# One written order for the first two parts of an input projection

## The chip, the cores and the metric

The kernel runs on one core of one Trainium2 chip. The metric is the device time of one execution in microseconds (us). Three runs of the kernel before took 2344.2, 2344.32 and 2345.24 us.

The engines are called as the profile calls them: PE (TensorE), DVE (VectorE), ACT (ScalarE), POOL (GpSimd) and SP (SyncE, which here only issues DMAs).

## The reference, cut to what matters

One step of a two-layer network for two groups of 128 tokens each: context tokens and latent tokens. Both groups have D_MODEL = 2048 features and share all parameters. They differ in a conditioning vector, from which a shift, a scale and a gate per feature are made for every sub-layer. The first layer begins like this:

```python
mod = jax.nn.silu(cond) @ w_ada[l] + b_ada[l]
sh1, sc1, gt1, sh2, sc2, gt2 = jnp.split(mod[:, None, :], 6, axis=-1)
h = rmsnorm(x, g_norm_mix[l]) * (1 + sc1) + sh1
...
proj = h @ w_in
q_lat, ckv, k_rope = proj[..., :i0], proj[..., i0:i1], proj[..., i1:i2]
```

`rmsnorm` divides each token by the root of the mean of its squares. `w_in` has 2048 rows and 2880 columns. Attention, an output projection, a gated feed-forward network with a convolution and a second layer follow; the change touches them only in a helper and through the scheduler.

## The kernel before, in words

**Layout.** Features lie on the 128 partitions, tokens along the free axis: `x` is 16 chunks of 128 features by 256 tokens, the first 128 of which are the context group. Each f32 product is made of three: an operand is split into a high part (rounded to fp32r by a cast on ACT) and a low part (the difference, on DVE), and PE multiplies high by high, low by high and high by low. `split` (L242 to L245) does this for weights; its ACT cast is the group "wh" (L244) in the profile, its DVE difference the group "wl" (L245). `gemm` (L330) issues the three matmuls for each chunk of rows into one of three PSUM banks called `acc`.

**The in-projection** is in `mixer_ab` (L825). Its 2048 rows are taken in five parts: chunks 0 and 1 (part one), chunks 2 and 3 (part two), and then three parts of four chunks. Each part runs over 23 columns of 128 outputs (`part`, L936). Part one copies its sums to SBUF on ACT (L942), the others add theirs on DVE (L944). A column of parts one and two is six matmuls, a column of the later parts twelve. `Weights` (L249) loads tiles of 1 MB (2048 values on each partition) into one of three buffers called `raw`; a tile holds eight columns of part one or two, or four of a later part.

**Shift and scale** are vectors made on PE. A *unit* is 512 features of one of them: four tiles of 1 MB of `w_ada`, summed against the conditioning (`sum_rows`), then turned onto the partitions with transposes and finished on DVE. `ROWS` (L70) lists the units in order of need; `pump` and `row_step` (L560, L529) place them between the columns of a part at a rate (`RATE["in0"]` in part two). The first unit of the scale (j = 1) and of the shift (j = 0) is done in two halves of two tiles each, with 256 features (`load_half` L359, `half_unit` L366), so that part one can begin with its two chunks. Their tiles lie in two buffers called `araw`, which the later units use as well, or in `raw`.

**The start** (L1300 on). All constants are loaded with one DMA, then `x` in four pieces, then the tiles of the first halves. `stat_add` squares the 16 chunks one at a time on ACT and adds them on DVE; `stat_rstd` sums over the partitions on PE with a one-column matmul and takes the root (DVE and POOL, `rstd` L202). `diagonal` (L228) puts the factor on two diagonal matrices on DVE, and `spread` (L235) multiplies them with ones on PE, so that the factor stands on every partition. `modulate` (L591) makes the rows of a part from that: a product on DVE, scale and shift for one group on DVE and for the other on ACT, a cast on ACT and the low part on DVE or POOL.

**What sets the order.** The program is written in an order, and a scheduler places each engine's instructions by its own estimate of time, except those given to `keep_order`, which stay in the written order among themselves on their engine. `pe.in_turn` does this for all of PE's instructions while it is set; before, it is set for the third and fourth part only. Each engine then executes its own list strictly in turn, and SP issues DMAs in turn: a DMA that waits for a buffer holds up all behind it. In part one of before, the second halves' tiles are loaded behind column 2 and column 8 and summed behind columns 8 and 15 (`second_half`, L953), where the scheduler may shift them.

Of the kernel before, what the change touches and what calls it, by code (L numbers as in the profile page):

```python
# [37 lines left out]
    ("ident", 128), ("ones", 128), ("pick", 32), ("inv", 5), ("mhalf", 16),  # L38
    ("rch", 128), ("rsh", 128), ("rcm", 128), ("rsm", 128),
    ("cond", 32), ("bada", NL * 6 * KD),  # L40
    ("gmix", NL * KD), ("gffn", NL * KD), ("gfin", 16),
# [9 lines left out]
RATE = {"in0": 0.35, "in": 0.5, "in3": 0.25, "heads": 0.85, "out0": 0.75, "c": 0.43, "outc": 0.43}  # L51
# [37 lines left out]
def step_kernel(ctx: ExitStack, tc: tile.TileContext, A: dict):  # L89
# [54 lines left out]
    sp.dma_start(out=cst, in_=A["cst"])  # L144
# [17 lines left out]
    pool.memset(condw, 0.0)  # L162
    act.activation(condw[:, :, 0:2], C("cond").rearrange("p (k r) -> p k r", r=2), AF.Silu)
# [64 lines left out]
    def diagonal(r, cols):  # L228
        dg = T_(tmp, [P, 2 * T], "diag", bufs=1)
        for i, c in enumerate(cols):  # L230
            dve.tensor_scalar(out=dg[:, i * T:(i + 1) * T], in0=ident, scalar1=r[:, c:c + 1],
                              scalar2=None, op0=ALU.mult)
        return dg
# [15 lines left out]
    class Weights:  # L249
# [9 lines left out]
        def load(self):  # L259
            raw = T_(wpool, [P, 4, 512], "raw").rearrange("p g n -> p (g n)")  # L260
            sp.dma_start(out=raw, in_=self.src[self.at])
            self.at += 1
            return raw

        def ahead(self, pin):

            if not self.half:
                self.half = [self.load(), 0]
            raw, lo = self.half
            self.blocks += self.halves(raw, lo, pin)  # L270
            self.half = None if lo else [raw, 8]

        def halves(self, raw, lo, pin=lambda i: i):
            wh = T_(wpool, [P, 1024], "wh", F32R, bufs=4)
            wl = T_(wpool, [P, 1024], "wl", F32R, bufs=4)
            for at in range(0, 8, FINE):
                s = slice(at * P, (at + FINE) * P)
                split(wh[:, s], wl[:, s], raw[:, (lo + at) * P:(lo + at + FINE) * P], pin)
            return [(wh[:, b * P:(b + 1) * P], wl[:, b * P:(b + 1) * P]) for b in range(8)]

        def chunk(self):
            while len(self.blocks) < self.nblk:
# [3 lines left out]
                n = self.per  # L286
                if self.cycle:
                    n = min(n, self.cycle - self.at * n % (-(-self.cycle // n) * n))
                n *= self.nblk if self.per < TB else 1
                raw = T_(wpool, [P, 4, 512], "raw").rearrange("p g n -> p (g n)")  # L290
                sp.dma_start(out=raw[:, :n * P], in_=self.src[self.at, :, :n * P])
                self.at += 1
# [16 lines left out]
    def first_three(W, xh, xl, order, mid=None, fixed=False):  # L309
# [3 lines left out]
        raws = [W.load() for _ in range(3)]  # L313
# [45 lines left out]
    def load_half(j, h, tag):  # L359

        raws = [T_(wpool, [P, 4, 512], tag, **({"bufs": 2} if tag == "araw" else {})) for _ in range(2)]
        for t, raw in enumerate(raws):
            sp.dma_start(out=raw, in_=A["w_ada"][0, j, 0, 2 * h + t])
        return [raw.rearrange("p g n -> p (g n)").rearrange("p (b n) -> p b n", b=8) for raw in raws]

    def half_unit(j, h, raws, pin=lambda i: i):  # L366
        ps = T_(ppool["ada"], [P, 512], "ada", bufs=1)
        for k in range(KD):
            g = k % 4
            pin(pe.matmul(ps[32 * g:32 * g + 32, :NT], condw[:, k, :], raws[k // 8][:, k % 8],  # L370
                          start=(k < 4), stop=(k >= KD - 4), skip_group_check=True))
        am = T_(tmp, [P, 512], "am", bufs=1)
        act.copy(am[:, :NT], ps[:, :NT])
        pt = T_(ppool["ada"], [P, 512], "ada", bufs=1)
        for b in range(2):
            pe.transpose(pt[:, b * P:(b + 1) * P], am[:, b * P:(b + 1) * P], ident)
        at = slice(2 * h, 2 * h + 2)
        out = mod[:, 0, j, at]
        dve.tensor_reduce(out=out, in_=pt[:, :NT].rearrange("p (b g r) -> p b r g", b=2, g=4)[:, :, 0:2],
                          axis=AX.X, op=ALU.add)  # L380
        dve.tensor_tensor(out=out, in0=out, in1=vector("bada", 0, j, 0)[:, at], op=ALU.add)
        if j == 1:
            dve.scalar_tensor_tensor(out=scl[:, 0, 0, at], in0=out, scalar=1.0,
                                     in1=vector("gmix", 0, 0, 0)[:, at], op0=ALU.add, op1=ALU.mult)
        if h == 1:
            done.add((0, j, 0))
# [105 lines left out]
    def side_step():  # L492
# [11 lines left out]
        sp.dma_start(out=block, in_=A["w_ada"][u[0], u[1], u[2], k // 4][:, k % 4])  # L504
# [82 lines left out]
    def norm_scale(st):  # L587
        return spread(diagonal(stat_rstd(st, D), (0, 1)))

    def modulate(hx, rb, l, which, chunks, fixed=False):  # L590
# [26 lines left out]
        for c, h in lows:  # L617
            low(c, h)

# [45 lines left out]
    def modulated(st, l, which, W, u, to, rp):  # L665
# [18 lines left out]
        def stats():  # L684
            got["r"] = stat_rstd(st, D, att_bank)
            got["dg"] = diagonal(got["r"], (0, 1))

        def factor():
            got["rb"] = spread(got["dg"], bank=att_bank)
# [135 lines left out]
    def mixer_ab(hx, rb0, beside):  # L825
# [658 lines left out]
```

## Time and profile before

| What | Value |
|---|---|
| runs, median of 3 | 2344.32 us |
| span of the profiled execution (first to last instruction) | 2343.4 us |
| PE busy | 2301.2 us, 98% |
| weight loads of PE (PEld) busy | 2182.7 us, 93% |
| DVE busy | 1852.7 us, 79% |
| ACT busy | 1194.5 us, 51% |
| DMA | 612.98 MB, mean 262 GB/s |
| granted PE clock, mean | 0.996 |

The page shows the span of the profiled execution and no other time of its own; the runs are 0.8 to 1.8 us longer than the span. The page divides the span into 40 slices of 58.6 us, and gives the busy share of each engine in tenths. A table of windows gives the same for any stretch in microseconds, with the number of records in brackets. The chain of waits follows back from the last instruction what released each step. A busy PE is not PE at its peak: a matmul is shown longer than the distance to the next one, and a stream of them is read from the distance. "PE acc", "PE ada", "PE misc" are matmuls into the PSUM banks of that name: projections, sums of `w_ada` (and their transposes), and statistics.

### The profile page before, as it was taken

To read this page: it belongs to the slowest core of one execution; us is meant where nothing else is said; L and a number is where in the kernel's file an instruction comes from. 1 tells how busy PE (TensorE), PEld (TensorE's weight loads), DVE (VectorE), ACT (ScalarE), POOL (GpSimd) and SP (SyncE) were. 2 spreads that over 40 slices of the span, in tenths; PEclk is the share of its full clock that TensorE was granted. 3 is DMA by queue.
4 is the path that set the end of the run, shared out by engine and by line. 5 is a ranking of instruction groups with operands and counts; after the bars stand their busy time and mean duration, and the time that the engine had idled before them with its cause. 6 is when DMAs were issued, how large, how long until landed. Compare 5 with 4: busy or idle time off the path is not lost.

```text
span 2343.4 us, 47891 instructions
## 1 busy us (share of the span) xinstructions
PE 2301.2 (98%) x19650; PEld 2182.7 (93%) x19650; DVE 1852.7 (79%) x2879; ACT 1194.5 (51%) x1979; POOL 177.4 (8%) x250
## 2 busy tenths in 40 slices
PE   6999999999999999999999999999999999999997
PEld 4788768999999999999989999999999999999997
DVE  3569767789999999999988888797899755666654
ACT  4245545575553355555564444456655434555543
POOL 0002101210000000001130000023000000000011
PEclk9999999999999999999999999999999999999999
DMA  9988888677767777777778888777677555555553
GB/s 367 358 326 290 305 320 331 231 285 259 262 253 290 293 266 266 270 260 261 284 272 287 308 307 293 259 261 257 243 260 267 196 198 191 189 196 198 194 189 122
DMA packets 106524, 612.98 MB, mean 262 GB/s; under 512 B 11520, under 2 KB 19392, under 8 KB 38592
## 3 DMA queue, kind: packets, MB, share of 16 engines
q1 hardware_dynamic: 106304, 609.92, 71.8%
q8 instruction: 154, 2.52, 0.4%
q14 instruction: 66, 0.54, 0.1%
HBM read 605.12 MB, written 4.75 MB: 260 GB/s over the span
## 4 chain that ended last, share of the span: by engine, by line
PE 94%; DVE 2%; DMA 2%; ACT 1%; issue 1%; POOL 0%; SPq 0%; DVEq 0%; ACTq 0%; POOLq 0%
PE acc L104 86%; PE ada L104 4%; PE att L104 2%; DMA raw<-w_in_ab 1%; PE att L107 1%; DMA araw<-w_ada 1%; DVE wl L245 1%; PE misc L104 1%; PE ada L107 0%; ACT wh L244 0%; POOL block L736 0%; DVE aacc L488 0%; DVE x L1348 0%; DVE nt L603 0%; ACT p L787 0%
## 5 line engine op out<-in xcount | busy, mean ns | idle before, releaser
L244 ACT CAST wh<-raw 128x1024 fp32r<-128x1024 f32 (+2 forms) x824 | 795.2, 976 | 938.6 <-PE acc L104 742.9
L104 PE MATMUL acc<-hx,wh 128*128 128x256 f32 (+1 forms) x7296 | 1260.5, 278 | 5.7 <-ACT hx L613 4.3
L245 DVE TENSOR_TENSOR wl<-raw,wh 128x1024 fp32r<-128x1024 f32 (+2 forms) x824 | 919.1, 1132 | 302.1 <-ACT wh L244 296.9
L104 PEld LDWEIGHTS acc<-hx,wh 128*128 128x128 f32 x7296 | 1102.3, 188 | 39.0 <-issue 19.2
L104 PE MATMUL acc<-hx,wl 128*128 128x256 f32 (+1 forms) x3648 | 1011.4, 278 | 4.5 <-DVE wl L245 4.5
L104 PEld LDWEIGHTS acc<-hx,wl 128*128 128x128 f32 x3648 | 686.4, 188 | 9.8 <-DVE wl L245 5.5
L104 PE MATMUL acc<-g,wh 128*128 128x256 f32 x2816 | 478.9, 276 | 0.0
L104 PEld LDWEIGHTS acc<-g,wh 128*128 128x128 f32 x2816 | 424.0, 188 | 0.0
L104 PE MATMUL acc<-g,wl 128*128 128x256 f32 x1408 | 388.6, 276 | 0.0
L459 DVE CUSTOM_DVE_ANT_0 junk<-araw,condb 128x2048 f32<-128x2048 f32 x120 | 275.9, 2299 | 0.0
L104 PE MATMUL acc<-hxc,wh 128*128 128x256 f32 (+1 forms) x1536 | 267.5, 278 | 1.1 <-DVE hxc L740 1.1
L104 PEld LDWEIGHTS acc<-g,wl 128*128 128x128 f32 x1408 | 264.3, 188 | 0.0
L104 PEld LDWEIGHTS acc<-hxc,wh 128*128 128x128 f32 x1536 | 233.0, 188 | 1.8 <-DVE hxc L740 1.3
L104 PE MATMUL acc<-hxc,wl 128*128 128x256 f32 (+1 forms) x768 | 218.4, 284 | 0.0
L200 POOL TENSOR_TENSOR sqacc<-sqacc,sq 128x256 f32<-128x256 f32 x62 | 68.5, 1105 | 1512.9 <-ACT sq L196 1512.6
L488 DVE SCALAR_TENSOR_TENSOR aacc<-block,condw,aacc 128x512 f32<-128x512 f32 x240 | 170.9, 747 | 7.4 <-DMA block<-w_ada 7.2
L104 PEld LDWEIGHTS acc<-hxc,wl 128*128 128x128 f32 x768 | 144.7, 188 | 15.8 <-issue 11.3
L104 PE MATMUL ada<-araw,condw 128*32 128x512 f32 (+1 forms) x736 | 94.2, 591 | 13.8 <-DMA araw<-w_ada 13.8
L1242 ACT ACTIVATE cv<-acc,convw 128x256 f32<-128x256 f32 x170 | 94.8, 557 | 0.0
L755 DVE SCALAR_TENSOR_TENSOR x<-acc,mod,x 128x128 f32<-128x128 f32 x192 | 57.8, 343 | 41.7 <-PE acc L104 41.6
L1248 DVE SCALAR_TENSOR_TENSOR cv<-acc,convw,cv 128x254 f32<-128x254 f32 x170 | 81.4, 479 | 3.3
L1245 DVE SCALAR_TENSOR_TENSOR cv<-acc,convw,cv 128x254 f32<-128x254 f32 x170 | 80.7, 475 | 0.0
(224 smaller groups left out, 1404.6 us busy)
## 6 DMA issues: line engine op xcount, KB each, us to landing
raw<-w_up SPq DMA_DIRECT2D x176, 1024.0 KB, 4.8
araw<-w_ada SPq DMA_DIRECT2D x146, 1024.0 KB, 5.4
raw<-w_down SPq DMA_DIRECT2D x88, 1024.0 KB, 4.8
raw<-w_in_c SPq DMA_DIRECT2D x48, 1024.0 KB, 6.5
block<-w_ada SPq DMA_DIRECT2D x128, 256.0 KB, 5.3
raw<-w_in_ab SPq DMA_DIRECT2D x19, 1024.0 KB, 7.5
raw<-w_out_ab SPq DMA_DIRECT2D x16, 1024.0 KB, 7.4
raw<-w_out_c SPq DMA_DIRECT2D x16, 1024.0 KB, 6.2
```

The source lines that it names most:

```text
L104: return self.placed(nc.tensor.matmul(*a, **kw))
L107: return self.placed(nc.tensor.transpose(*a, **kw))
L200: eng.tensor_tensor(out=st["acc"], in0=st["acc"], in1=sq, op=ALU.add)
L244: pin(act.copy(out_hi, src))
L245: pin(dve.tensor_tensor(out=out_lo, in0=src, in1=out_hi.bitcast(F32), op=ALU.subtract))
L459: keep_order(dve.tensor_tensor_reduce(out=T_(feat["pool"], [P, D], "junk"), in1=feat["row"][:, c], in0=feat["raw"].rearrange("p g n -> p ( ...
L488: i = dve.scalar_tensor_tensor(out=acc[c], in0=block, scalar=condw[:, k, c:c + 1], in1=acc[c], op0=ALU.mult, op1=ALU.add)
L755: dve.scalar_tensor_tensor(out=x[:, c, s], in0=ps[:, s], scalar=mod[:, l, 3 * which + 2, c, g:g + 1], in1=x[:, c, s], op0=ALU.mult, op1=AL ...
L1242: pin(act.activation(y, ps, AF.Identity, scale=cw[:, 1, m:m + 1], bias=cw[:, 3, m:m + 1]))
L1245: pin(dve.scalar_tensor_tensor(out=y3[:, :, 1:], in0=p3[:, :, :T - 1], scalar=cw[:, 0, m:m + 1], in1=y3[:, :, 1:], op0=ALU.mult, op1=ALU.add))
L1248: pin(dve.scalar_tensor_tensor(out=y3[:, :, :T - 1], in0=p3[:, :, 1:], scalar=cw[:, 2, m:m + 1], in1=y3[:, :, :T - 1], op0=ALU.mult, op1=A ...
```

## The change

It rewrites the start and the first two parts of the in-projection.

- The fields of the constants are put in another order; 373 columns are loaded first, the other 1024 inside part one, behind column 10 (`late_constants`).
- A dummy Silu on ACT stands ahead of the real one.
- The squares are taken four chunks at a time: four ACT instructions of 128x1024 and three DVE additions of that size, and eight one-column matmuls where there were four.
- `diagonal` is gone. `spread` multiplies the factor, broadcast along its row as the stationary operand, with the identity: two matmuls of 128x128 in place of one of 128x256. All callers use it: the first norm, the latents' and keys' norms, the two places of `modulated`, and the last norm.
- `half_unit` becomes the class `HalfUnit` with separate steps (`sums` of a tile, `copy`, `turn`), all kept in order, its sums and its transposes in PSUM banks of their own.
- The rows of parts one and two are made in two steps: `scaled_rows` (product with the factor and with the scale, DVE) as soon as the scale is there, and `begin_row` (shift and cast in one ACT instruction per group, low part on DVE) once the shift is there.
- `Weights` gets `begin` (load ahead, in order) and `take`. The loads of `w_ada` and `w_in_ab` at the start are all kept in order on SP, and so are the blocks of `side_step`, which before could be loaded at any time.
- `pe.in_turn` is set from part one on. The second halves' tiles are summed behind columns 4 and 10 (scale) and 15 and 19 (shift); the loads of the shift's tiles stand behind the first two of these.
- `RATE["in0"]` is 0.42 in place of 0.35, and `pump` runs from column 20 of part one in place of 16.

The core of the diff:

```diff
-RATE = {"in0": 0.35, ...
+NEARLY = _AT["bada"][0] + 2 * KD
+RATE = {"in0": 0.42, ...
-    sp.dma_start(out=cst, in_=A["cst"])
+    sp.dma_start(out=cst[:, :NEARLY], in_=A["cst"][:, :NEARLY])
+
+    def late_constants():
+        keep_order(sp.dma_start(out=cst[:, NEARLY:], in_=A["cst"][:, NEARLY:]))
...
-    def spread(dg, cols=(0, 1), bank=bank):
+    def spread(r, bank=bank):
         ps = bank()
-        n = len(cols) * T
-        pe.matmul(ps[:, :n], ones, dg[:, :n], start=True, stop=True)
-        return ps[:, :n]
+        for g in range(2):
+            pe.matmul(ps[:, g * T:(g + 1) * T], r[:, g:g + 1].to_broadcast([P, P]), ident, start=True, stop=True)
+        return ps[:, :NT]
...
-                for h in range(2):
-                    W = Weights(A["w_in_ab"][3 * h:3 * h + 3], 2, 8, cycle=23)
-                    if h == 0:
-                        W.ahead(keep_order)
-                    modulate(hx, rb0, 0, 0, range(2 * h, 2 * h + 2))
-                    if h == 0:
-                        part(W, 0, 2, True, 0, second_half)
-                    else:
-                        part(W, 2, 2, False, RATE["in0"], until=4)
+                def second_half(c):
+                    if c == 0:
+                        W0.ahead(keep_order)
+                    elif c == 4:
+                        second["u"] = HalfUnit(1, 1, ppool["first"], att_bank)
+                        second["u"].sums(0, second[1][0])
+                        second[0] = load_half(0, 1, "araw", (0,))
+                    elif c == 10:
+                        second["u"].sums(1, second[1][1])
+                        second["u"].copy()
+                        second[0] += load_half(0, 1, "araw", (1,))
+                        halves.begin(2)
+                        late_constants()
+                    elif c == 11:
+                        second["u"].turn()
+                    elif c == 15:
+                        second["u"] = HalfUnit(0, 1, ppool["first"], att_bank)
+                        second["u"].sums(0, second[0][0])
+                        second["nt"] = scaled_rows(rb0, 2, 2)
+                    elif c == 19:
+                        second["u"].sums(1, second[0][1])
+                        second["u"].copy()
+                    elif c == 20:
+                        second["u"].turn()
+                        for i, h in enumerate(second["nt"]):
+                            begin_row(hx, h, 2 + i)
+                    if c >= 20:
+                        pump(RATE["in0"], until=4)
+
+                second[1] = load_half(1, 1, "araw", (0,))
+                W0.begin()
+                second[1] += load_half(1, 1, "araw", (1,))
+                W0.begin()
+
+                def first_half(c):
+                    if c == 20:
+                        rest.begin()
+
+                pe.in_turn = True
+                part(W0, 0, 2, True, 0, second_half)
+                part(halves, 2, 2, False, RATE["in0"], first_half, then=lambda: rows(1), until=4)
...
-        half_unit(1, 0, first[1], keep_order)
-        st = stat_init()
-        for c in range(KD):
-            stat_add(st, x[:, c], KD, dve)
-        rb0 = norm_scale(st)
-        half_unit(0, 0, first[0], keep_order)
+        W0 = Weights(A["w_in_ab"][0:3], 2, 8, cycle=23)
+        W0.begin(2)
+            for i in range(4):
+                to = sums if i == 0 else T_(sqs, [P, 4, NT], "sqs", bufs=2)
+                keep_order(act.activation(to, x[:, 4 * i:4 * i + 4], AF.Square))
+                if i:
+                    keep_order(dve.tensor_tensor(out=sums, in0=sums, in1=to, op=ALU.add))
+            unit = HalfUnit(1, 0, ppool["first"], att_bank)
+            unit.sums(0, first[1][0])
+            ps = bank()
+            for g in range(2):
+                for i in range(4):
+                    keep_order(pe.matmul(ps[:, g:g + 1], sums[:, i, g * T:(g + 1) * T], inv(D),
+                                         start=(i == 0), stop=(i == 3)))
+            r = rstd([ps[:, 0:2]], 2)
+        unit.sums(1, first[1][1])
+        unit.copy()
+        rb0 = spread(r)
+        unit.turn()
+        nts = scaled_rows(rb0, 0, 2)
+        unit = HalfUnit(0, 0, att_bank, att_bank)
+        for t in range(2):
+            unit.sums(t, first[0][t])
+        W0.ahead(keep_order, rows)
```

In the program as built, SP's list at the start reads: early constants, `x` (four), the scale's first two tiles (`araw`), the shift's first two (`raw`), part one's first tile in two pieces, the scale's third tile, part one's second, the scale's fourth, part one's third, the shift's third, the shift's fourth, part two's first tile in two pieces, the late constants, and four tiles of the next unit (two in `raw`, two in `araw`), then part two's second tile. PE's list has the sums of that unit's first tile, which is the third of the four on SP's list, ahead of part two's first column. From there on SP's list differs from the old one only in the place of the side blocks and in some neighbours changing places.

More of the change, by code (lines that the diff above doesn't have):

```diff
@@ L285, in chunk @@
                     continue
[L286 to L292, printed above, removed]
+                raw, n = self.take()
                 n0 = FINE if fine[0] else 8
@@ L312, in first_three @@
         pin = keep_order if fixed else lambda i: i
-        raws = [W.load() for _ in range(3)]
+        raws = [W.load()[0] for _ in range(3)]
         ps = [T_(pacc, [P, 512], "acc") for _ in range(3)]
@@ L357, in step_kernel, with load_half @@
     later = []
[L359 to L363, printed above, removed]
+    def load_half(j, h, tag, tiles=(0, 1)):
+        raws = [T_(wpool, [P, 4, 512], tag, **({"bufs": 2} if tag == "araw" else {})) for _ in tiles]
+        for t, raw in zip(tiles, raws):
+            keep_order(sp.dma_start(out=raw, in_=A["w_ada"][0, j, 0, 2 * h + t]))
@@ L364, in load_half @@
         return [raw.rearrange("p g n -> p (g n)").rearrange("p (b n) -> p b n", b=8) for raw in raws]
[L366 to L386, printed above, removed]
@@ L822, in head_ab, with mixer_ab @@
         split(hx[:, c, :NT], hx[:, c, NT:2 * NT], o[:, :NT])
-    def mixer_ab(hx, rb0, beside):
+    def mixer_ab(hx, rb0, W0, beside):
         l = 0
@@ L978, in rows @@
                     modulate(hx, rb0, 0, 0, range(4 * q, 4 * q + 4))
-                rows(1)
+                halves, more, second = Weights(A["w_in_ab"][3:6], 2, 8, cycle=23), {}, {}
+                rest = Weights(A["w_in_ab"][6:], 4, 4, cycle=23)
+                def second_half(c):
[36 more added lines that the diff above has]
+                part(halves, 2, 2, False, RATE["in0"], first_half, then=lambda: rows(1), until=4)
+                W = rest
                 for q in range(1, 4):
```

132 lines of the change are left out of this document (92 added, 40 removed).

## The prediction

> **What bounds the kernel now.** I read the page's 40 slices first, then a table of windows cut at the parts of the in-projection, then the chain of waits and the timeline inside the early windows.
>
> ```profile
> PE   6999999999999999999999999999999999999997
> DMA  9988888677767777777778888777677555555553
> ```
> ```profile
> 0.00:28.00 28.00, 11.26 (x78) 5.61 (x78) 10.71 (x31) 11.45 (x27) 1.41 (x6) 1.00 0.95 377
> 28.00:53.00 25.00, 23.63 (x206) 19.24 (x206) 9.81 (x18) 14.54 (x34) 1.22 (x1) 0.93 0.98 388
> 53.00:82.50 29.50, 26.52 (x212) 19.02 (x212) 19.00 (x47) 10.88 (x20) 2.72 (x3) 1.00 0.95 382
> 82.50:130.00 47.50, 45.54 (x357) 37.18 (x358) 28.15 (x52) 16.03 (x23) 1.63 (x2) 0.96 0.84 309
> 174.50:214.00 39.50, 38.86 (x328) 36.53 (x327) 39.38 (x83) 24.33 (x54) 10.70 (x11) 1.00 0.79 269
> 214.00:350.00 136.00, 134.60 (x935) 101.27 (x938) 101.49 (x254) 69.91 (x166) 18.11 (x47) 1.00 0.85 315
> 480.00:600.00 120.00, 120.00 (x1058) 120.00 (x1057) 108.80 (x148) 72.31 (x100) 0.00 (x0) 1.00 0.72 261
> ```
>
> The columns are the length, then busy us and records of PE, weight loads, VectorE, ScalarE and GpSimd, then granted clock, DMA share and GB/s. PE has no idle time from 480 to 600 us, and nine tenths or more in every slice but the first and last: only the start, the stages up to 480 us and the tail have time to give. The changed stretch is 0 to 82.5 us. There the DMA engines are 95 to 98% busy, so loads bound it together with PE's order. In 174.5 to 214 VectorE is full (39.38 of 39.50).
>
> **The change part by part.** First the prices of PE work, from the chain of waits and the timeline (an f32 matmul leaves two records there, so x16 is eight):
>
> ```profile
> 12.67 1.94 PE ada L104 x16
> 14.60 1.80 PE misc L104 x8
> 44.34 1.00 PE ada L104 x16
> 53.91 1.75 PE acc L104 x12
> 62.98 2.07 PE acc L104 x18
> 82.86 4.39 PE acc L104 x22
> ```
> ```profile
> 18.19 1.22 PE L104 MATMUL misc<-diag,cst 128*128 128x256 f32 x2
> 19.21 0.64 PE L107 MATMUL ada<-cst,am 128*128 128x128 f32 x2
> 21.01 3.64 PE L104 MATMUL ada<-raw,condw 128*32 128x256 f32 x32 [1.16 <-DVE mod L379]
> 28.34 1.01 PE L104 MATMUL acc<-hx,wh 128*128 128x256 f32 x3 [2.71 <-ACT hx L613]
> 31.15 0.58 PE L104 MATMUL acc<-hx,wh 128*128 128x256 f32 x1
> 59.23 1.04 PE L104 MATMUL ada<-raw,condw 128*32 128x512 f32 x8
> ```
>
> One tile of half-unit sums is 1.94 us when PE is slow and 1.00 when fast; a projection matmul is 0.115 fast (2.07/18) and 0.20 slow (4.39/22), so a column of parts one and two (six matmuls) is 0.69 or 1.2. One tile of a whole unit's sums is 1.0.
>
> Then the loads, from windows of 2.5 us and the view of the tile `araw`:
>
> ```profile
> 5.00:7.50 2.50, 0.00 (x0) 0.00 (x0) 0.43 (x1) 2.30 (x6) 0.00 (x0) 1.00 1.00 379
> 32.50:35.00 2.50, 2.50 (x29) 1.79 (x29) 0.00 (x0) 1.39 (x4) 0.00 (x0) 1.00 1.02 421
> 80.00:82.50 2.50, 0.72 (x7) 0.52 (x5) 2.50 (x7) 1.08 (x2) 0.62 (x1) 1.00 1.01 416
> 82.50:85.00 2.50, 2.14 (x10) 2.15 (x11) 1.77 (x3) 0.00 (x0) 0.00 (x0) 0.59 0.20 82
> ```
> ```profile
> DMA to landing us min/median/max: 4.8/9.4/13.2
> ```
>
> A full queue moves about 0.425 MB/us, so a tile of 1.05 MB takes 2.47 us of it. Alone, such a tile lands 4.8 us after its issue: 2.3 us more, of which I put 0.9 behind the data.
>
> *Start.* Only 373 of the 1397 columns of constants stand ahead of x. That is 0.52 MB or 1.2 us less, so the first half-unit tile lands at 11.4 where it landed at 12.67, and x, one tile ahead of it, at 9.0. The squares become four of 128x1024 on ScalarE and three such additions on VectorE; the trace has neither, and the nearest rows are casts and differences:
>
> ```profile
> 34.54 2.00 ACT L244 CAST wh<-raw 128x1024 fp32r<-128x1024 f32 x2 [0.63 <-DMA raw<-w_in_ab]
> 35.62 2.36 DVE L245 TENSOR_TENSOR wl<-raw,wh 128x1024 fp32r<-128x1024 f32 x2 [5.27 <-ACT wh L244]
> ```
>
> At 1.0 and 1.2 us the last ones end at 11.2, hidden behind the tile; half the price or twice it, they stay hidden, since PE sums until 13.4 first. PE then has, in its written order: sums 1.94 (to 13.4), eight one-column matmuls where it had four (3.6, to 17.0), sums 1.94 (18.9; the root is taken beside it), two spreading matmuls with the factor itself as stationary operand (bounds 0.64 and 1.22; I take 1.0), two transposes 0.64 (20.5), two tiles of the shift's sums 3.64 (24.2). Before, these ended at 24.65: 1.8 us of added matmuls eat the saved 1.2 us and the wait on the diagonals. What follows:
>
> ```profile
> 24.77 0.37 ACT L373 COPY am<-ada 128x256 f32<-128x256 f32 x1 [6.07 <-PE ada L104]
> 25.88 0.16 DVE L381 TENSOR_TENSOR mod<-mod,cst 128x4 f32<-128x4 f32 x1
> 26.57 0.60 DVE L609 TENSOR_SCALAR nt<-nt,scl,mod 128x128 f32<-128x128 f32 x2
> 27.12 0.88 ACT L612 ACTIVATE nt<-nt,mod,scl 128x128 f32<-128x128 f32 x2
> 27.90 0.70 ACT L613 CAST hx<-nt 128x256 fp32r<-128x256 f32 x2
> ```
>
> From copy to sum is 1.3 us (25.5); four half rows at 0.44 on ScalarE end at 27.3 and the last low part, 0.3, at 27.6. Column 0 ends at 28.2. Before, PE's steady run began at 31.15, with 1.94 us of sums done ahead of it.
>
> *Part one.* Columns 1 and 2 slow (2.4), 3 and 4 fast, sums: 33.0. Six columns and sums: 38.1. Twelve columns 8.3, two sums 2.0, two turns with the wait on their copies 1.5: 49.9. The row of before is
>
> ```profile
> 52.38 0.37 ACT L942 COPY qb<-acc 128x256 f32<-128x256 f32 x1 [0.51 <-PE acc L104]
> ```
>
> so part one is over some 2.3 us sooner.
>
> *Loads ahead of part two.* Here the gain goes. SP's order is written now: the scale's second half and part one's two other tiles in turn; the shift's second half, whose tiles wait for the sums behind column 4 (33.0) and column 10 (38.1), because `araw` has two buffers; then part two's first tile in halves, the late constants, three tiles of the next unit. All behind waits in line on SP. The queue runs dry near 31 for some 4 us and again for 2.6. From 38.2 the waiting tile's data ends at 38.2+4.8-0.9=42.1; 4.7 MB stand behind it up to the last of those three, 11.1 us: data at 53.2, landed at 54.1. That last one, in `araw`, is the unit's first, and PE's order puts its sums ahead of part two's column 0. The rows of part two are ready at 51.0, but PE stands from 49.9 to 54.1. Before, part two began at 53.91.
>
> The halves and the constants are three pieces of 0.5 MB in that line. With x's pieces of this size the window 5.00:7.50 shows 379 GB/s, 0.15 us more a piece; unhidden, a piece pays the 2.3 us. I take 0 and keep 2.3 for the range. The Trainium skill, "DMA: Bandwidth & Descriptors", sections Anatomy of one DMA and Bandwidth, speaks against such pieces: a fixed time of about 2.0 us for each transfer, and a rule to move 1 MiB or more at once. By it alone, unhidden, the sum would be 6 us worse; the x row shows a tenth of that under a full queue, so this is a rival below and not the forecast.
>
> *Part two.* A stall of 2.1 us ahead of 82.86 left PE slow (clock 0.59), one of 1.6 us ahead of 53.91 hardly (1.75/12=0.146). After 4.2 us I count the first sums at 1.94 and columns 0 and 1 at 2.1 together. The other 21 columns are 14.5, seven sums 7.0, two turns 1.2: 54.1+1.9+2.1+22.7=80.8. The loads keep up: six tiles and one of 0.92 MB behind 53.2 are 17.0 us, so part two's third tile lands at 71.1, is split by 73.3 and is needed at 74.4. Before, PE ended near 80.7 (0.72 busy in 80.00:82.50). Even.
>
> *Into part three.*
>
> ```profile
> 78.64 1.98 POOL L598 TENSOR_TENSOR hx<-nt,hx 128x256 fp32r<-128x256 f32 x2 [23.65 <-ACT hx L613]
> 80.93 0.74 DVE L603 TENSOR_TENSOR nt<-x,misc 128x256 f32<-128x256 f32 x2
> 81.59 1.21 DVE L245 TENSOR_TENSOR wl<-raw,wh 128x1024 fp32r<-128x1024 f32 x1
> ```
>
> Here the split of part three's first tile stood behind products for rows not yet needed, and PE waited. Now they stand behind it. But the rows are later: their unit is turned at 77.4, then ScalarE has four scalings 1.8, a cast 1.0 and four copies 1.4 (82.1), GpSimd the last low part (83.4). Column 1 ends at 85.2, against 82.86+4.39=87.2: 2.0 gained (bounds 0, if the rows come as late as the split did, and 3.8, if stall and slow clock both go).
>
> *The rest.* SP's order is nearly the old one from here, so part three's waits shift along. Two products for diagonals (0.48 together) leave VectorE three times in 174.5 to 214: 0 to 1.4, I take 0.7. At the end:
>
> ```profile
> 2332.31 0.48 DVE L231 TENSOR_SCALAR diag<-cst,rr 128x128 f32<-128x128 f32 x2 [0.81 <-POOL rr L211]
> 2332.94 1.19 PE L104 MATMUL misc<-diag,cst 128*128 128x256 f32 x2 [1.64 <-DVE diag L231]
> ```
>
> 0.5 us off the path. The heads' instructions are shuffled; PE idles only 1.4 of 136 us there: 0, give or take 3.
>
> Sum: 2.0+0.7+0.5=3.2 us less. The profiled span is 2343.4, and the runs' median 2344.3 lies 0.9 above it: **2341.1**.
>
> **The rivals.** *The wait is hidden (faster).* If the tile of 54.1 lands with the rows at 51.0 and PE stays fast, column 16 comes 4.7 us sooner; part two's third tile, 3.1 sooner too, binds at 70.2, so 4.2 are gained: 2336.9. For it: over 6 us of idle DMA, which an earlier column 4 or 10 shortens. Against it: SP waits in line behind two buffers.
>
> *The loads never run full (slower).* The sum needs 11.9 MB between 42.1 and 70.2. At the 309 GB/s of 82.50:130.00 they take 38.5 us instead of 28.1; less 1.1 of slack that is 9.3 lost: 2350.4. It turns the sign below 0.37 MB/us. For it: each tile waits for sums that wait, in PE's fixed order, for the tile before. Against it: 382 in 53.00:82.50.
>
> *Short pieces pay their fixed time.* At 1.1 us each the gain is gone; at the 2.3 of a load alone, with nothing beside it, the time is 2341.1+6.9=2348.0.
>
> **How the numbers follow.** Forecast (2339.6 to 2344) 0.43, hidden wait 0.30, slow loads 0.16, short pieces 0.11. A measurement can tell about 0.2%, 4.7 us, from no change. The hidden wait lies beyond that, with an edge of the forecast; slow loads too; the rest is inside: faster 0.31, same 0.53, slower 0.16. The range reaches over both outer cases' prices, less their far ends: 2334 (with 3 us from the heads) to 2350.
>
> **What would show it.** Right: PE idle some 4 us near 50, ended by an `araw` load; DMA gaps near 32 and 38; part two over near 81; no stall on the split there. Wrong: part two begun by 52 or after 57, or under 0.37 MB/us between 42 and 70. What would break it is a first column ending before 27 or after 30: every load behind columns 4 and 10 moves with it.

## The result, and the profile after

Six runs of the changed kernel took 2351.69 to 2360.82 us, median 2356.36; the kernel before took 2344.87 beside them. The ratio is 1.0042, with a 95% interval of 1.0032 to 1.0052: slower by some 10 us, where 2341.1 was forecast. The profiled execution took 2357.61, with a span of 2355.8 against 2343.4.

*Where it is lost.* The table of windows, as for the kernel before:

```profile
0.00:28.00 28.00, 13.16 (x96) 8.37 (x97) 8.48 (x21) 9.10 (x15) 1.42 (x6) 1.00 0.91 348
28.00:53.00 25.00, 21.05 (x201) 17.59 (x199) 13.34 (x28) 16.10 (x37) 0.00 (x0) 1.00 0.88 342
53.00:82.50 29.50, 26.15 (x185) 17.06 (x186) 12.29 (x27) 5.90 (x7) 0.00 (x0) 0.88 0.93 362
```

Read the last column first: 348, 342 and 362 GB/s where the kernel before had 377, 388 and 382. Up to 82.5 us that is 2.6 MB less moved, which is 6 us of a queue at 0.425 MB/us. Of these, 0.8 MB are the three side blocks, which the kernel before loads from 7.49 us on and the changed one only from 157.26 us on, so the first row shows no loss by itself. PE's busy time shrinks in the second and third row, and its clock, 1.00 in 53 to 82.5 before, is 0.88.

The ends of the parts are read from their last sums, `qb` on VectorE (for part one the last copy on ScalarE). In the timeline of the kernel before, for parts two to five:

```profile
82.73 0.41 DVE L944 TENSOR_TENSOR qb<-qb,acc 128x256 f32<-128x256 f32 x1
130.24 0.41 DVE L944 TENSOR_TENSOR qb<-qb,acc 128x256 f32<-128x256 f32 x1
173.40 0.41 DVE L944 TENSOR_TENSOR qb<-qb,acc 128x256 f32<-128x256 f32 x1
213.48 0.41 DVE L944 TENSOR_TENSOR qb<-qb,acc 128x256 f32<-128x256 f32 x1
```

and in that of the changed kernel, part one first:

```profile
50.47 0.62 ACT L982 COPY qb<-acc 128x256 f32<-128x256 f32 x2
...
85.44 1.07 DVE L984 TENSOR_TENSOR qb<-qb,acc 128x256 f32<-128x256 f32 x3
138.21 0.41 DVE L984 TENSOR_TENSOR qb<-qb,acc 128x256 f32<-128x256 f32 x1
184.70 0.41 DVE L984 TENSOR_TENSOR qb<-qb,acc 128x256 f32<-128x256 f32 x1
225.56 0.41 DVE L984 TENSOR_TENSOR qb<-qb,acc 128x256 f32<-128x256 f32 x1
```

A row's start and length give its end. Part one ends 1.7 us sooner (51.09 against 52.75), part two 3.4 later, part three 8.0, part four 11.3, part five 12.1. Behind part five both kernels take the same: 2343.4 - 213.9 = 2129.5 and 2355.8 - 226.0 = 2129.8. So the whole loss is made in parts two to four and a little in five, and what lies behind part five takes the same in sum. These sums can lag behind PE, as VectorE has other work in its list: PE's last matmul of part two ends at 80.5 before and at 85.6 in the changed kernel, 5.1 us later.

*Parts one and two.* SP's own timeline (the second column holds the time of the issues with the waits between them), then windows:

```profile
31.83 5.76 SPq L372 DMA_DIRECT2D araw<-w_ada  x2
37.70 0.85 SPq L268 DMA_DIRECT2D raw<-w_in_ab  x2
38.59 0.65 SPq L148 DMA_DIRECT2D cst<-cst  x1
39.34 0.92 SPq L563 DMA_DIRECT2D raw<-w_ada  x2
42.51 4.27 SPq L563 DMA_DIRECT2D araw<-w_ada  x2
49.00 0.33 SPq L268 DMA_DIRECT2D raw<-w_in_ab  x1
57.43 0.33 SPq L563 DMA_DIRECT2D araw<-w_ada  x1
```
```profile
32.00:36.00 4.00, 4.00 (x36) 4.00 (x34) 1.84 (x2) 2.63 (x8) 0.00 (x0) 1.00 0.82 305
36.00:40.00 4.00, 3.92 (x40) 3.00 (x39) 3.01 (x7) 2.88 (x6) 0.00 (x0) 1.00 0.40 111
53.00:60.00 7.00, 4.56 (x20) 2.87 (x20) 0.42 (x1) 0.00 (x0) 0.00 (x0) 0.56 0.97 378
60.00:70.00 10.00, 9.83 (x76) 6.17 (x78) 5.87 (x13) 2.59 (x3) 0.00 (x0) 0.97 0.86 320
```

The two `araw` loads of the first row wait for PE's sums behind columns 4 and 10, and all later loads wait in line behind them: in 36 to 40 the queue moves 111 GB/s. PE pays at 55.44:

```profile
55.44 1.94 PE L105 MATMUL ada<-araw,condw 128*32 128x512 f32 x8 [5.30 <-DMA araw<-w_ada]
...
88.63 0.58 PE L105 MATMUL acc<-hx,wh 128*128 128x256 f32 x1 [2.27 <-DVE hx L620]
```

It stands 5.30 us and is slow behind that (clock 0.56 in 53 to 60). Then comes a second round: between 49.33 and 57.43 SP issues nothing, because the next load's buffer is the one that these late sums still hold, and in 60 to 70 the loads drop to 320 GB/s. The second row of PE's timeline above is the way into part three, with a stall of 2.27 and a slow clock again (0.50 in 88.6 to 91.1).

### The profile page after: what moved, and what is told of

The parts are those of the page before. It is cut to its first block, busy times and chain, and to the rows that moved or that the text cites. A ratio compares the mean times of both kernels' runs of the same rounds, so it can differ in the third digit from the quotient of the medians.

```text
span 2355.8 us, 47863 instructions
## 1 busy us (share of the span) xinstructions
PE 2305.4 (98%) x19674; PEld 2187.8 (93%) x19674; DVE 1852.7 (79%) x2862; ACT 1192.4 (51%) x1968; POOL 182.4 (8%) x248
## 4 chain that ended last, share of the span: by engine, by line
PE 94%; DMA 3%; DVE 2%; ACT 1%; issue 0%; SPq 0%; POOL 0%; DVEq 0%; ACTq 0%
PE acc L105 86%; PE ada L105 4%; PE att L105 2%; DMA araw<-w_ada 2%; PE att L108 1%; DVE wl L244 1%; PE misc L105 1%; DMA raw<-w_in_ab 1%; PE ada L108 0%; DVE aacc L510 0%; ACT wh L243 0%; DMA block<-w_ada 0%; DVE x L1437 0%; DVE proj L984 0%; DVE ql L901 0%
```

## The experiments

**Theory 1**: the loss is the wait for that one tile, and what follows from its late, slow clock. **Theory 2**: parts four and five have a loss of their own, from the pinned blocks and the lists that shift with them. **Theory 3**: the wait covers other loads that are late anyway. Two more theories came later. **Theory 4**, from the first four runs: parts one and two are bound by bytes, and each microsecond in which the queue is held back comes out at part two's end. **Theory 5**, from the three runs after these: short first pieces move slower.

The runs came in four sets, each with the kernel before beside it. A ratio compares a kernel with that one, and its interval is 2 to 4 us wide to each side, so most single steps below are no larger than the noise; profiles are of one execution each.

**The first unit's buffers swapped** (`a_unit_raw`).

```diff
-            if ada["i"] < 8 and t % 2:
+            if ada["i"] < 8 and t % 2 != (ada["i"] == 2):
```

> The changed kernel, with the two sets of buffers swapped for the tiles of the first whole unit, so that the tile whose sums PE takes ahead of part two's column 0 is the first of that unit on SP's list and not the third. Theory 1 (the loss begins at PE's wait for that tile, 5.3 us, and what follows in parts two and three is its late and slow clock): the wait falls under 1 us, part two begins near 51 instead of 55.4 and column 1 of part three ends near 88 instead of 93.9; if this is all of the loss, the time is 2344 to 2346. Theory 2 (the lists of ScalarE and VectorE and the pinned side blocks of part four are a loss of their own, 3.3 us there and 4.1 by part five's end): the wait goes as well, but part four gives nothing back: 2349 to 2351. Theory 3 (the wait hides others, loads that are late in any case): column 1 of part three still ends after 92, 2354 to 2357.

Measured: 2353.75 (2349.89 to 2354.89), ratio 1.0036 [1.0023, 1.0049]. PE's timeline:

```profile
50.89 1.06 PE L105 MATMUL ada<-raw,condw 128*32 128x512 f32 x8 [0.32 <-DMA raw<-w_ada]
...
55.79 1.10 PE L105 MATMUL ada<-araw,condw 128*32 128x512 f32 x8 [2.26 <-DMA araw<-w_ada]
```

The wait goes from 5.30 to 0.32 and part two begins 4.5 us sooner, but its next tile is late in turn, and its last sum ends at 85.31 against 86.51. Theory 1 is refuted as the whole cause: by the medians only 2.6 us come back, by the ratios 1.4, and the two intervals overlap. The time lies between the forecasts of theories 2 and 3. By the profiled execution, the fastest of the five, part three is as quick as theory 1 had it (47.7 us from last sum to last sum, 52.1 in the changed kernel, 47.5 before), though its column 1 ends at 90.7, between the 88 of theory 1 and the 92 of theory 3. Part four gives little back (45.1, against 46.5 in the changed kernel and 43.2 before), much as theory 2 had it. That part two still ends after 85 is theory 3's.

**The blocks' loads unpinned** (`b_blocks_free`).

```diff
-        keep_order(sp.dma_start(out=block, in_=A["w_ada"][u[0], u[1], u[2], k // 4][:, k % 4]))
+        sp.dma_start(out=block, in_=A["w_ada"][u[0], u[1], u[2], k // 4][:, k % 4])
```

> The changed kernel, with the loads of the side unit's blocks no longer pinned in the written order, so that the first three of them move up on SP's list to the first tiles, as they stood before the change. The same edit lets ScalarE's list in part four put the casts of a w_in tile ahead of a unit's copy that waits for PE. Theory 2 (part four's loss is of its own): the first 130 us stay as in the changed kernel, the 3.3 us of part four and 0.8 of part five come back, 2351 to 2353. Theory 1 (all comes from the wait at part two): no change beyond 1 us, 2355 to 2357.

Measured: 2352.35, 1.0031 [1.002, 1.0043], inside theory 2's 2351 to 2353. Theory 2 also had the first 130 us stay as they were, and they didn't: part two's last sum ends 1.6 us later (88.12), and part three takes 49.1 us for 52.1. The mechanism is read in part four. ScalarE and PE in the changed kernel, then SP:

```profile
169.83 0.59 ACT L437 COPY am<-ada 128x512 f32<-128x512 f32 x1 [8.36 <-PE ada L105]
170.31 3.46 ACT L243 CAST wh<-raw 128x1024 fp32r<-128x1024 f32 x4
171.41 0.50 PE L105 MATMUL acc<-hx,wh 128*128 128x256 f32 x2 [1.70 <-ACT wh L243]
```
```profile
157.26 0.95 SPq L526 DMA_DIRECT2D block<-w_ada  x2
```

ScalarE idles 8.36 us for a copy that waits for PE, with the casts that PE needs next queued behind it; PE stands 1.70 us for the first of them and 0.76 us for its low part. With the loads unpinned:

```profile
166.69 1.99 ACT L243 CAST wh<-raw 128x1024 fp32r<-128x1024 f32 x2 [6.60 <-DMA raw<-w_in_ab]
168.59 0.58 ACT L437 COPY am<-ada 128x512 f32<-128x512 f32 x1
```

The casts stand first, and PE's one stall there is 0.46 us, at 169.05. From part to part, by the last sums, part four takes 43.9 us (46.5 in the changed kernel, 43.2 before) and part five 39.3 (40.9, 40.1). The other runs agree: 45.1 to 45.6 and 40.3 to 40.9 in the three with pinned blocks (the swap, `h_fill`, `r_const_only`), 42.8 to 45.3 and 39.3 in the seven others without, where only the one with blocks in part three is over 44.1. Three pairs of kernels differ by this edit alone: this one and the changed kernel, both edits and the swap, `j_fill_free` and `h_fill` (below). By their ratios it is worth 2.6, 3.5 and 3.8 us. Whether it is SP's list or ScalarE's that does it, these runs don't separate.

**Both edits** (`g_raw_and_free`).

> The changed kernel with both edits: the first unit's buffers swapped and the blocks' loads unpinned. If theories 1 and 2 are each right and independent, the gains add: some 7 and 4 us, 2344 to 2347. If something else holds parts two to five as well, it stays above 2349. If the start's 2.3 us then come through to the end: 2342 to 2344.

Measured: 2349.62, 1.0021 [1.0012, 1.0031]. Within the noise the gains add, and some 5 us stay lost. This and the swap's late second tile led to theory 4.

**Only the start, on the kernel before** (`c_before_start`): constants split, squares in four chunks, all else as before.

```diff
...
-        st = stat_init()
-        for c in range(KD):
-            stat_add(st, x[:, c], KD, dve)
-        rb0 = norm_scale(st)
...
+            sums = T_(sqs, [P, 4, NT], "sqsum")
...
+                act.activation(to, x[:, 4 * i:4 * i + 4], AF.Square)
...
+            rb0 = spread(diagonal(rstd([ps[:, 0:2]], 2), (0, 1)))
```

> The kernel before, with only the start changed: constants split (the late ones behind the second half's tiles), squares four chunks at a time. Diagonals, half units, order of loads and of PE's work as before. If the start's gain of about 2 us holds through to the end: 2342 to 2343. If it is taken up by part one's loads, which bind there: 2344 to 2345. If the split constants or the squares cost where they stand: 2346 or more.

Measured: 2348.78, 1.0021 [1.0011, 1.0031], slower. The scheduler put the one-column matmuls ahead of the first tile's sums:

```profile
13.31 3.57 PE L105 MATMUL misc<-cst,sqsum 128*128 128x1 f32 x16 [13.31 <-DVE sqsum L1317]
```

So the first `araw` buffer came free later. SP's next pair of loads, first in this run, then in the kernel before:

```profile
18.81 2.04 SPq L367 DMA_DIRECT2D araw<-w_ada  x2
```
```profile
14.65 4.00 SPq L363 DMA_DIRECT2D araw<-w_ada  x2
```

The pair begins 4.2 us later, and part two's last sum ends 4.8 us later (87.98 against 83.14). So in the old order of loads too, a buffer given back late seems to cost its delay about once; a part of it may be the split constants' (below), which this run doesn't separate.

**Loads moved into the dry stretch** (`h_fill`).

```diff
                 W0.begin()
+                halves.begin(2)
+                late_constants()
...
                         second[0] += load_half(0, 1, "araw", (1,))
-                        halves.begin(2)
-                        late_constants()
```

> The changed kernel, with part two's first tile and the late constants (1.57 MB) begun ahead of the shift's second half instead of behind its second tile: they wait for no sums of PE, so they can move while the queue was dry (near 32 to 40 us). Theory 4, formed on the swap of buffers (there the wait for the first tile fell from 5.3 to 0.3 us and part two still ended at 84.9 against 85.4): parts one and two are bound by bytes, and each microsecond in which the loads are held back is lost at part two's end. Then the 1.57 MB, 3.7 us at 0.425 MB/us, come back: 0.00:85 moves more GB/s, part two ends at 81 to 82, the time is 2351 to 2353. Theory 1 (the wait for the unit's first tile alone): that tile still waits for the sums behind column 15, so nothing changes by over 1 us, part two ends at 85, 2355 to 2357.

Measured: 2353.11, 1.0028 [1.0019, 1.0037].

```profile
36.00:40.00 4.00, 3.92 (x40) 3.14 (x40) 3.20 (x4) 3.66 (x8) 0.00 (x0) 1.00 1.03 430
53.00:60.00 7.00, 4.54 (x24) 2.98 (x28) 3.33 (x5) 1.86 (x2) 0.00 (x0) 0.76 0.65 242
```

The stretch is filled (430 for 111 in 36 to 40), but SP's list now holds part two's second tile ahead of the unit's tile whose sums PE takes first, PE waits 3.81 us for that at 55.46, and the queue runs dry behind the wait instead (242). Part two's last sum ends at 86.74, not at 81 to 82. The time is at theory 4's edge; the place where it should show was missed. By the last sums, what this run gains lies in part three (44.5 us for 52.1).

**Filled and unpinned** (`j_fill_free`), **all three edits** (`k_fill_raw_free`).

> The same, with the blocks' loads unpinned as well. Theory 4 with theory 2 (part four's own loss comes from the pinned blocks and the lists that they shift): both gains, 2347 to 2349; unpinned alone gave 2352.35. Theory 1: as unpinned alone, 2351 to 2353.

> All three edits: part two's first tile and the late constants begun ahead, the first unit's buffers swapped, the blocks' loads unpinned. Theory 4: with no tile waiting for sums ahead of what is needed first, the queue runs full nearly throughout, part two ends at 80 to 81 as before the change or sooner, column 1 of part three ends by 87, and the time is 2342 to 2345. If the order of loads isn't the cause, it stays at the 2349.6 of the swap with the unpinned blocks.

Measured: 2347.91, 1.0012 [1.0003, 1.0022], and 2346.85, 1.0001 [0.9992, 1.001]. The first is inside the 2347 to 2349 of theories 2 and 4 together, but its part two still ends at 87.85, so the place was missed here too. With all three the loss is gone, though without the gain that theory 4 allowed. By the ratios, the swap was worth 1.4, 2.3 and 2.6 us in the three pairs that differ by it alone, and the filled stretch 3.3, 4.5 and 4.7; each of these is uncertain by some 3 us, but the sum of the three edits, 9.6, is well outside the noise. One window over the stage up to 82.5 us puts the kernels beside each other. In order: the kernel before, the changed one, all three edits, and the last experiment below.

```profile
0.00:82.50 82.50, 61.40 (x496) 43.87 (x496) 39.52 (x93) 36.87 (x79) 5.35 (x10) 0.98 0.96 382
```
```profile
0.00:82.50 82.50, 60.36 (x479) 43.02 (x480) 34.11 (x75) 31.10 (x59) 1.42 (x6) 0.96 0.91 351
```
```profile
0.00:82.50 82.50, 62.46 (x505) 46.24 (x505) 38.63 (x84) 35.26 (x68) 1.90 (x7) 0.98 0.96 380
```
```profile
0.00:82.50 82.50, 64.78 (x536) 47.66 (x536) 42.21 (x94) 35.35 (x69) 3.60 (x8) 1.00 0.98 394
```

Part two's last sum ends at 83.14, 86.51, 83.29 and 80.83. In all 14 kernels it ends at or before 83.3 where the window moved 377 GB/s or more, and after 85 where it moved 364 or less. That the two go together doesn't say which causes which: a late PE also gives its buffers back late.

**The blocks loaded in part three** (`n_blocks_mid`): on all three edits, a function issues the first three blocks, pinned, behind column 18 of part three.

> The version with all three edits, with the side unit's first three blocks (0.79 MB, not needed before part five) loaded in part three, where the DMA engines have time, instead of among the first tiles. Theory 4 (parts one and two are bound by bytes): 1.9 us of the queue come free ahead of part two, so the two waits of PE on unit tiles in part two (1.32 and 1.98 us) shrink, part two ends near 81 instead of 83, and the time is 2344 to 2346 instead of 2346.85. If parts one and two are no longer bound by bytes once the gaps are filled: part two ends at 83 as before, 2346 to 2348.

Measured: 2347.72, 1.0006 [0.9996, 1.0015]: no gain, against theory 4. Without the blocks the queue moves 315 GB/s from 20 to 28 us, where it moved 412 with them: they had filled a stretch in which the list waits anyway. The two waits of PE for unit tiles did shrink, from 1.32 and 1.98 us to 0.69 and 0.55, but PE then stands 2.24 us at 78.02 for a copy that ScalarE makes behind two casts (shown in the last section), and part two's last sum ends at 82.86, for 83.29. So fewer bytes alone brought nothing here; that the waits of the queue bind, and not its bytes, fits this but isn't shown by it.

**Constants in one piece** (`p_const_whole`) and **first tiles whole** (`q_whole_tiles`), each on all three edits.

```diff
-    sp.dma_start(out=cst[:, :NEARLY], in_=A["cst"][:, :NEARLY])
+    sp.dma_start(out=cst, in_=A["cst"])
```
```diff
-                halves.begin(2)
+                halves.begin()
...
-        W0.begin(2)
+        W0.begin()
```

> The version with all three edits, with the constants loaded in one piece at the front again (0.72 MB), nothing late. By the prediction's step, 0.52 MB more ahead of x land the first half-unit tile 1.2 us later than the 13.23 of this version, at 14.4. By theory 5 (a queue of the short first pieces runs at some 300 GB/s where the whole constants beside them gave 375 to 379, so the split brings the landing nothing): it lands at 12.7 to 13.2, and the window from 32 to 36 us, without the late piece, moves more than 322 GB/s. Time 2345 to 2348 either way.

> The version with all three edits, with the first tiles of parts one and two loaded whole instead of in halves. Theory 5 (short pieces move slower even with the queue full, 264 to 328 GB/s from 33 to 36 us against 438 behind them): that stretch gets shorter by about 1 us, with 380 GB/s or more where no late constants stand; the first split of part one may start later by the second half's landing (at most 1.2 us, with PE busy until 24). Rival (the low rate is the time between two issues, or other queues): the same rate as before. Time 2345 to 2348 either way.

In the first, nothing is loaded late any more. Measured: 2342.23, 0.9983 [0.9974, 0.9993], and 2346.15, 1.0003 [0.9994, 1.0013]. Whole constants are worth 4.6 us here (4.2 by the ratios), more than either theory allowed, and the first tile lands at 12.67, as in the kernel before, with 0.52 MB more ahead of it. By the last sums only 1.5 us are gained by part two's end. Part three then takes 44.5 us for 48.7: with all three edits PE stalls 1.61 us on its way into part three and its clock is 0.67 in 85 to 90 us, and here the trace has no such stall, and the clock is 1.00. The edit also takes the late piece out of the line near 32 us, so it doesn't tell which end of the split cost. Whole tiles raise 32 to 36 us from 322 to 368 GB/s; their time can't be told from no change.

**Constants in one piece on the changed kernel alone** (`r_const_only`), and **everything** (`s_whole_all`: all three edits, whole constants, whole tiles).

> The changed kernel with one edit: the constants in one piece at the front again, nothing late. Theory 5 (the split slows the first 10 us of the queue): the first half-unit tile lands at 12.7 instead of 13.09 with 0.53 MB more moved by then, part two's first tile and the units' tiles land some 1.2 us sooner (the late piece is out of their line); together 2 to 3 us, 2353 to 2354.5. If the split was worth as much as in the version with all edits (4.6 us): 2351 to 2352.5. By the prediction's step (1.2 us later landing, made good in the line later): no change, 2355 to 2357. The gaps of the queue near 32 and 38 us stay, so it must not come under 2350.

> The version with all three edits, with the constants in one piece and the first tiles of parts one and two whole. The constants alone gave 2342.23 and whole tiles 2346.15 against 2346.85. If short pieces cost by themselves (theory 5): 2340.5 to 2342. If the split tiles serve (the first split of part one begins sooner): 2342.5 to 2344.

Measured: 2355.57, 1.004 [1.0024, 1.0055]: no gain to be seen, and the median is outside both of theory 5's ranges, but with four runs a gain of 2 to 3 us lies inside the interval. By the profile the loads start faster (380 GB/s in 2.5 to 5 us, 297 in the changed kernel), the first tile lands at 13.11, no sooner than before the edit, and the loads then wait all the longer (124 GB/s in 32 to 36, 305 in the changed kernel). And everything together: 2340.25 (2339.62 to 2344.48), 0.9978 [0.997, 0.9987], **faster than both kernels**. Its windows:

```profile
2.50:5.00 2.50, 0.00 (x0) 0.00 (x0) 0.00 (x0) 0.23 (x1) 0.00 (x0) 1.00 1.00 391
...
32.00:36.00 4.00, 3.70 (x33) 3.50 (x32) 2.36 (x2) 2.88 (x8) 0.00 (x0) 1.00 1.02 425
36.00:40.00 4.00, 3.49 (x36) 2.58 (x35) 2.20 (x4) 3.68 (x8) 0.00 (x0) 1.00 1.02 424
```

No dry stretch is left, and the ends of the parts are 50.4, 80.8, 124.4, 168.0 and 207.4.

## Why the prediction was wrong

**What held.** PE's chain at the start; in kind, the dry queue "near 31" and again behind column 10, though it was milder than forecast (223 and 226 GB/s in 32 to 34 us, 8 and 0 in 36 to 38); the start of that pair of loads (31.83 and 37.3; forecast 33.0 and 38.1), part one's end (its last matmul at 50.1; forecast 49.9), and PE standing ahead of part two for the first unit's tile, found in the order and not in the diff. It was forecast to end at 54.1 and ended at 55.44.

**The landing, 11.4.** The first tile landed at 13.09, later than before, though less stood ahead of it. The changed kernel's windows:

```profile
2.50:5.00 2.50, 0.00 (x0) 0.00 (x0) 0.00 (x0) 0.23 (x1) 0.00 (x0) 1.00 0.97 297
5.00:7.50 2.50, 0.00 (x0) 0.00 (x0) 0.00 (x0) 1.06 (x1) 0.00 (x0) 1.00 0.99 354
```

and the first of these in the kernel before (379 from 5 to 7.5 us stands in the prediction):

```profile
2.50:5.00 2.50, 0.00 (x0) 0.00 (x0) 0.00 (x0) 0.13 (x1) 0.00 (x0) 1.00 1.00 375
```

I took the saved bytes at the full rate; the rate fell with them. In the nine profiles with split constants that show it, the tile lands at 12.47 to 13.76, and in the four with whole ones at 12.67 to 13.11, so the saved bytes don't show. PE made most of this good: its sums for the shift took 2.47 us, where I counted the 3.64 of before, and they ended at 24.38, where I had 24.2.

**Part two "even".** This is the step that failed first. I let the loads run full from 42.1 to 70 ("the loads keep up") right behind a stall that I had forecast. But the stall keeps the next buffers: `araw` was given back at 57.4, and SP stood for 8 us. The window, in the changed kernel and then in the kernel before:

```profile
42.00:70.00 28.00, 21.52 (x165) 14.67 (x158) 10.94 (x24) 8.22 (x17) 0.00 (x0) 0.88 0.95 366
```
```profile
42.00:70.00 28.00, 26.20 (x227) 19.23 (x226) 11.68 (x26) 10.10 (x22) 0.74 (x1) 1.00 0.91 349
```

At 0.366 MB/us the stretch gives 10.2 MB where 11.9 were needed. That is just under the rate at which I let the second rival turn the sign, and the mechanism is the one that I wrote under it: each tile waits for sums that wait for the tile before. By that rival's own sum, 11.9 MB at 0.366 take 32.5 us in place of 28.1, and less the 1.1 of slack that is 3.3 lost; with the 1.3 by which part two began late it makes 4.6, and PE ended part two at 85.6 where I had 80.8. Its 309 GB/s was too low for this stretch, and I gave it a chance of only 0.16. The rate by itself isn't low: the kernel before moved less in these 28 us. But that one had moved 392 GB/s up to 42 us, and the changed one, with its dry stretches and without the side blocks, 331; it had something to make good, and I let it do so at a rate that the held buffers didn't allow.

**Into part three, 2.0 gained.** The split no longer stood behind the products, as written; instead the low parts of the rows stood behind the second split:

```profile
86.44 1.27 DVE L244 TENSOR_TENSOR wl<-raw,wh 128x1024 fp32r<-128x1024 f32 x1
87.63 1.27 DVE L620 TENSOR_TENSOR hx<-nt,hx 128x256 fp32r<-128x256 f32 x2
```

PE's stall there was 2.27 (2.14 before) and its clock slow again. From the end of part two on PE to the end of column 1 it took 8.2 us (6.7 before), so that 1.5 were lost, and column 1 ended at 93.8 where I had 85.2. I priced the wait removed and did not go on down VectorE's list to the next one.

**"SP's order is nearly the old one from here, so part three's waits shift along."** Wrong: by the last sums 4.6 us more in part three (of which 1.4 lie behind its column 1), 3.3 in part four, 0.8 in part five. With the buffers swapped part three was back at 47.7, which suggests that its loss came with part two's. In part four, the side blocks, once loaded early, were pinned into part four's line; I had read that pin in the diff and gave it no price. Unpinning alone is worth 4.0 us by the medians and 2.6 by the ratios.

**Short pieces.** As a fixed time of 1.1 to 2.3 us each they weren't seen: making the tiles whole again changed nothing measurable. As a rate the cost is there (264 to 328 GB/s from 33 to 36 us with all three edits, 438 from 37 on), and the constants' split costs 4.6 us where nothing else holds the queue. The Trainium skill, "DMA: Bandwidth & Descriptors", section Bandwidth, was right in its direction: move large pieces (both of its figures that I used are given there for transfers issued from GpSimd, and these are issued from SP). I had answered it with the one window, 379 GB/s, in which x's short pieces moved behind whole constants; behind split ones, in the two windows above, the pieces moved at 297 and 354.

**Diagonals and tail, -1.2; heads, 0.** Part five, where 0.7 should have come from the diagonals, took 0.8 longer. Behind it the two kernels differ by 0.3 us in sum, so the 0.5 of the tail could not be seen either.

## What to carry to other kernels

In a stage bound by its loads, a written order is a claim on buffers: go down the DMA queue's list and ask of each entry which sums give back its buffer, and what waits in line behind it. A stall that you forecast also holds buffers, so the stage behind it can't be counted at the full rate. Keep what needs no buffer from a slow consumer ahead of what does, and pin only what the order needs: the same rewritten parts, with another order and larger pieces of their loads, took 2340 instead of 2356.

## What was not expected of the hardware

- With the constants split, all ten profiles show 254 to 299 GB/s from 2.5 to 5 us; with one piece of 0.72 MB, all four show 375 to 391. The DMA engines were 0.84 to 0.99 busy in the former, 0.99 to 1.00 in the latter, so a part of the difference is idle time, and on average the larger part lies in how fast busy engines moved. The reason stays open. The constants' rows of 1.5 KB instead of 5.6 KB per partition weren't tried by themselves, and they had landed by 3.12 us in the changed kernel, so that most of what moved slowly there were x's pieces behind them.
- By the medians, whole constants gave 0.8 us on the changed kernel and 4.6 where the dry stretches were gone. Both figures are uncertain by some 3 us or more, so it isn't shown that gains don't add. The profiles fit it: in the changed kernel the faster start only lengthened a wait that is set by something else.
- The length of a stall alone doesn't tell whether PE's clock falls. Stalls of 2.26 and 2.27 us (the swap and the changed kernel) were followed by a slow clock (0.50 in 57 to 60 and in 88.6 to 91.1), but one of 2.24, with the blocks in part three, was not:

```profile
78.02 0.66 PE L108 MATMUL ada<-cst,am 128*128 128x128 f32 x4 [2.24 <-ACT am L437]
```
```profile
78.00:80.00 2.00, 1.99 (x17) 1.99 (x18) 1.91 (x6) 0.06 (x1) 0.00 (x0) 1.00 1.04 430
```

With all three edits, one of 1.61 was, after 1 us at full speed (timeline, then window):

```profile
83.68 0.39 PE L105 MATMUL acc<-hx,wh 128*128 128x256 f32 x1 [1.61 <-DVE hx L620]
```
```profile
85.00:87.50 2.50, 2.50 (x14) 2.50 (x13) 0.77 (x3) 1.99 (x2) 0.00 (x0) 0.50 0.74 292
```
